# Six more load buffers in the expert stage of a two-layer trunk, except around the expert with split weights

## The chip, the core and the metric

The kernel runs on one core of a Trainium2 chip. The metric is the device time of one launch in microseconds, the median of several runs. The engines in what follows are PE (matmuls) with its weight load PEld, DVE, ACT and POOL (element-wise work), and SP, which here only issues DMAs and reads a few registers. Weights come from HBM by DMA and land in SBUF buffers.

## What is computed

The reference is a trunk of two layers on 256 tokens of width 1024. Each layer has a mixer (an mLSTM group beside an RG-LRU group) and a channel mixer: a dense SwiGLU in layer 0, eight experts in layer 1, of which each token uses two. The part that the change touches is the last:

```python
def _swiglu(h, w_gate, w_up, w_down):
    return (jax.nn.silu(h @ w_gate) * (h @ w_up)) @ w_down

def _moe(h, w_router, b_router, w_g, w_u, w_d):      # h 256 x 1024
    logits = (h @ w_router + b_router).astype(jnp.float32)
    top_v, top_i = lax.top_k(logits, TOP_K)           # 2 of 8
    top_p = jax.nn.softmax(top_v, axis=-1)
    gates = jnp.sum(jax.nn.one_hot(top_i, 8) * top_p[..., None], axis=-2)
    y = jnp.zeros_like(h)
    for e in range(8):                                # w_g[e], w_u[e] 1024 x 2816, w_d[e] 2816 x 1024
        y = y + gates[..., e:e + 1] * _swiglu(h, w_g[e], w_u[e], w_d[e])
    return y
```

All is float32; the eight experts hold 264 MiB of weights, and each weight is read once.

## The kernel before

**Units.** The weights are worked off in units of 128 x 2048 floats, 1 MiB (768 KB for the gate and up units of the last chunk of a tiled expert). The expert stage has 278 of them, numbered here from 0. `moe_units` (L551) lists them: for each expert and each chunk of its 2816 inner columns (1024, 1024, 768, or six chunks in the B expert) the gate units, the up units, and then the down units of the chunk before. PE works through them in this order: `gate_up` (L1459) and `down` (L1543) call `take` (L505) for each unit.

**Kinds.** `KINDS = "MSBMSMMS"` says how many tokens each expert may take: S 64, M 96, B 128. In S and M experts the matmuls read the loaded floats as they are (gate and up at L1471 in an S, L1478 in an M; down at L1580 in an S, L1561 in an M). Only expert 2, the B, uses split weights: `split` (L356) makes a high part `hi` on ACT and a low part `lo = raw - hi` on DVE, each 128 x 2048 floats, and PE makes three products of them (L1483 to L1485 for gate and up, L1583 to L1585 for down). Its units are 67 to 110 (those up to 75 mixed with the last downs of expert 1). Layer 0 and both mixers, before the expert stage, also use split weights, from a pool that is closed when the stage opens.

**Buffers.** A load goes into a buffer of `rawp` (6, `LOADS`) or, in the expert stage, of `rawx` (4, `EXTRA`). The pool `xs` has 3 buffers for `hi` and 3 for `lo`. All are of one size. `raws` (L320) lists the pools that loads may use, each with the number of its buffers and the units that it has taken. `fill` (L468) emits loads as long as a pool has room: a pool has room if the unit that used its next buffer is done with, which `free` (L465) decides, for a unit used as it is (work `whole`) by whether PE's instructions for it stand in the program, for a split unit by whether its split does. `advance` (L488) calls `fill` and splits up to two units ahead. So the order in which instructions are emitted decides which buffer a load takes and which wait it carries.

**Queues.** Each engine works through its instructions in order. The loads (one DMA for nearly every unit, L335) all stand on SP; a load whose buffer is still read blocks all behind it. It also waits on the semaphore (DMAHW0 to 7, in turn) of the DMA eight before it. Seven reads of expert numbers into registers (`places`, L1330, tile `eid`) stand on SP as well, since the address of an expert's weights from expert 1 on depends on the routing, and one read of `cnt` (L1777), which says whether some token found no place; the branch that handles that is not taken here.

The pools of the stage open at L1811:

```python
    with tc.tile_pool(name="ex", ...) as ep, tc.tile_pool(name="xs", bufs=3, ...) as xs, tc.tile_pool(name="rawx", bufs=EXTRA, ...) as rawx:
        raws.append((rawx, EXTRA, []))
        rt["splits"] = xs
        fill()
        moe(1, ep)
```

Of the kernel before, what the change touches and what calls it, by code (L numbers as in the profile page):

```python
# [8 lines left out]
F32 = mybir.dt.float32  # L9
# [7 lines left out]
P = 128  # L17
# [16 lines left out]
LOADS, SPLITS, EXTRA = 6, (2, 2, 2, 2), 4  # L34
# [90 lines left out]
def trunk(ctx: ExitStack, tc: tile.TileContext, I, out, dbg=None):  # L125
# [12 lines left out]
    rawp = ctx.enter_context(tc.tile_pool(name="rawp", bufs=LOADS))  # L138
# [177 lines left out]
    units, state = [], {"load": 0, "work": 0, "take": 0, "limit": 1 << 30, "phase": 0}  # L316
# [2 lines left out]

    raws = [(rawp, LOADS, [])]  # L320

    def load(ap, shape, pool=rawp):
        raw = pool.tile([P, 2048], F32, tag="raw", name="raw")
        if isinstance(ap, list):
            v = raw[:, :shape[0] * shape[1]].rearrange("p (a b) -> p a b", a=shape[0])
            for i, x in enumerate(ap):
                nc.sync.dma_start(v[i * 64:(i + 1) * 64], x)
            return v
        if len(shape) == 3:
            v = raw.rearrange("p (a b c) -> p a b c", a=shape[0], b=shape[1])  # L330
            for c in range(shape[0]):
                nc.sync.dma_start(v[:, c], ap[:, c])
            return v
        v = raw[:, :shape[0] * shape[1]].rearrange("p (a b) -> p a b", a=shape[0])
        nc.sync.dma_start(v, ap)  # L335
        return v
# [124 lines left out]
    def run_tails(upto_):  # L461
        while tails and tails[0][0] <= upto_:
            tails.pop(0)[1]()

    def free(j):  # L465
        return j < (state["take"] if units[j]["work"] is whole else state["work"])

    def fill():  # L468
        while state["load"] < len(units):
            room = [r for r in raws if len(r[2]) < r[1] or free(r[2][-r[1]])]  # L470
            if not room:
                break
            u = units[state["load"]]
            u["raw"] = load(u["ap"]() if callable(u["ap"]) else u["ap"], u["shape"], room[0][0])
            room[0][2].append(state["load"])
            state["load"] += 1
            n = len(vectors) if state["load"] <= 4 else 0
            for _ in range(min(5, n)):
                vectors.pop(0)()

    def work(n):
        for _ in range(n):
            u = units[state["work"]]
            u["work"](u)
            state["work"] += 1
            fill()

    def advance(i):  # L488
        while True:
            fill()  # L490
            if state["work"] >= min(state["load"], i + 1 + SPLITS[state["phase"]], state["limit"]):
                break
            work(1)
# [735 lines left out]
    def moe(l, ep):  # L1229
# [398 lines left out]
        def general(ov, e, xn, j):  # L1628
# [26 lines left out]
            for c0, n in groups["B"]:  # L1655
                res = []
                for nm in ("w_exp_gate", "w_exp_up"):
                    ps = bank("ps_gu2")
                    kk = 4 if n == 512 else 8
                    for k0 in range(0, KD, kk):  # L1660
                        w = I[nm][0, bass.ds(e, 1), k0 * P:(k0 + kk) * P, c0:c0 + n]
                        raw = load(w.rearrange("o (k p) f -> p (o k) f", p=P), (kk, n))
                        for i in range(kk):
                            TE.matmul(ps[:, :n], xg[:, k0 + i, :], raw[:, i, :], start=k0 + i == 0,
                                      stop=k0 + i == KD - 1)
                    res.append(ps)
                a = ov.tile([P, 512], F32, name="a2", tag="a2")
                S.activation(a[:, :n], res[0][:, :n], AF.Silu)
                V.tensor_mul(a[:, :n], a[:, :n], res[1][:, :n])
                pt = bank("ps_t2")  # L1670
                for c in range(n // P):
                    TE.transpose(pt[:, c * P:(c + 1) * P], a[:, c * P:(c + 1) * P], ident)
                aT = ov.tile([P, 512], F32, name="aT", tag="aT")
                V.tensor_copy(aT[:, :n], pt[:, :n])
                for f0 in range(c0, c0 + n, 256):
                    w = I["w_exp_down"][0, bass.ds(e, 1), f0:f0 + 256, :]
                    raw = load(w.rearrange("o (k p) f -> p (o k) f", p=P), (2, D))
                    for c in range(2):
                        f = f0 + c * P
                        for h2 in range(2):  # L1680
                            TE.matmul(yo[h2], aT[:, f - c0:f - c0 + P], raw[:, c, h2 * 512:(h2 + 1) * 512],
                                      start=f == 0, stop=f == DFF - P)
# [126 lines left out]
    splits[0].__exit__(None, None, None)  # L1809
    prep.__exit__(None, None, None)  # L1810
    with tc.tile_pool(name="ex", bufs=1, reuse_waits="tile") as ep, tc.tile_pool(name="xs", bufs=3, reuse_waits="tile") as xs, tc.tile_pool(name="rawx", bufs=EXTRA, reuse_waits="tile") as rawx:  # L1811
        raws.append((rawx, EXTRA, []))
        rt["splits"] = xs
        fill()
        moe(1, ep)
# [28 lines left out]
```

## Time and profile before

| | us |
|---|---|
| runs | 1250.68, 1253.91, 1261.38 |
| median | 1253.91 |
| profiled execution | 1259.08 |
| its span in the trace | 1257.3 |
| mean granted clock of PE over the span | 0.972 |
| PE busy | 1178.8 (94% of the span) |
| DVE, ACT busy | 591.9 (47%), 374.8 (30%) |
| loaded from HBM | 397.67 MB, 317 GB/s over the span |

The expert stage runs from about 490 us to the end. In the profile a busy row gives an engine, the line of the kernel, the operation, `out<-in` with the names of the tiles (buffer numbers left out), and, in brackets, how long the engine was idle before it and which instruction or DMA released it; `issue` means that nothing in the trace did. The granted clock is a share of full speed: 1.00 is 2.4 GHz, 0.50 is 1.2 GHz. A row that holds several instructions (x8) gives the time from the first one's start to the last one's end. Matmuls overlap by some tenths of a microsecond, so the distance of two units is read from the start of one to the start of the next.

### The profile page before, as it was taken

How to read it: one execution, taken by the hardware profiler on the slowest of the kernel's cores; microseconds unless marked ns; L12 is line 12 of the kernel's file. 1: busy time of each engine (PE TensorE's matmuls, PEld its weight loads, DVE VectorE, ACT ScalarE, POOL GpSimd, SP SyncE). 2: the span in 40 equal slices, each digit the busy share in tenths (PEclk: the TensorE clock that was granted, in tenths of full speed). 3: DMA queues.
4: the chain of work that ended last, by engine and by line, in shares of the span. 5: the costliest groups of instructions: out<-in, count | busy, mean ns of one | idle time of the engine just before them, and what ended most of it. 6: DMA issues, size and time to landing. Idle time of an engine off the chain costs nothing.

```text
span 1257.3 us, 27066 instructions
## 1 busy us (share of the span) xinstructions
PE 1178.8 (94%) x11763; PEld 889.2 (71%) x11763; DVE 591.9 (47%) x992; ACT 374.8 (30%) x576; POOL 20.7 (2%) x51
## 2 busy tenths in 40 slices
PE   2999999999999998999997999999998999899994
PEld 2899989999999988666544688757534576567531
DVE  6899889898669974211013588220100101010122
ACT  3482564443458542102002477100000001000101
POOL 4000000000010000000000000000000000000000
PEclk9999999999999998899998899999999999999998
DMA  9986749999847646598999999889999999999994
GB/s 307 345 261 231 256 172 371 364 312 329 269 126 239 210 154 234 215 327 336 343 404 400 394 393 398 314 303 386 356 405 408 408 404 374 359 320 398 343 404 172
DMA packets 152557, 400.54 MB, mean 319 GB/s; under 512 B 6920, under 2 KB 56384, under 8 KB 152432
## 3 DMA queue, kind: packets, MB, share of 16 engines
q1 hardware_dynamic: 151872, 397.59, 87.1%
q8 instruction: 94, 1.54, 0.5%
q0 software_dynamic: 560, 1.16, 0.3%
q14 instruction: 31, 0.25, 0.1%
HBM read 397.67 MB, written 1.05 MB: 317 GB/s over the span
## 4 chain that ended last, share of the span: by engine, by line
PE 84%; DMA 11%; ACT 2%; DVE 2%; issue 1%; SPq 0%; DVEq 0%; ACTq 0%
PE ps_y L1561 10%; PE ps_g L1478 6%; PE ps_gu L1478 6%; PE ps_z L663 6%; PE ps_z L662 6%; PE ps_z L664 6%; PE ps_u L1478 6%; DMA raw<-in_w_exp_gate_dram 4%; PE ps_g L1471 4%; PE ps_u L1471 3%; PE ps_acc L662 2%; PE ps_acc L664 2%; DMA raw<-in_w_exp_up_dram 2%; PE ps_acc L663 2%; PE ps_acc L835 2%; PE ps_xg L1446 2%
## 5 line engine op out<-in xcount | busy, mean ns | idle before, releaser
L114 DVE TENSOR_TENSOR lo<-raw,hi 128x2048 fp32r<-128x2048 f32 x93 | 211.2, 2286 | 41.0 <-ACT hi L114 25.1
L114 ACT CAST hi<-raw 128x2048 fp32r<-128x2048 f32 x92 | 174.5, 1904 | 90.5 <-PE ps_acc L663 26.5
L662 PE MATMUL ps_z<-hh,hi 128*128 128x256 f32 x624 | 176.6, 285 | 1.4 <-ACT hi L114 1.3
L663 PE MATMUL ps_z<-hl,hi 128*128 128x256 f32 x624 | 176.1, 283 | 0.1
L664 PE MATMUL ps_z<-hh,lo 128*128 128x256 f32 x624 | 175.2, 283 | 0.0
L1478 PE MATMUL ps_gu<-raw,xf 128*32 128x256 f32 (+1 forms) x1536 | 124.3, 364 | 2.8 <-issue 2.8
L114 DVE SCALAR_TENSOR_TENSOR a<-a,gs,ps_u 128x256 f32<-128x256 f32 (+3 forms) x39 | 20.5, 551 | 223.4 <-PE ps_u L1478 108.0
L1561 PE MATMUL ps_y<-raw,aT 128*32 128x256 f32 (+1 forms) x1584 | 121.5, 451 | 0.0
L662 PEld LDWEIGHTS ps_z<-hh,hi 128*128 128x128 f32 x624 | 118.9, 191 | 2.1 <-ACT hi L114 1.7
L663 PEld LDWEIGHTS ps_z<-hl,hi 128*128 128x128 f32 x624 | 118.8, 190 | 0.7 <-DVE hl L114 0.5
L664 PEld LDWEIGHTS ps_z<-hh,lo 128*128 128x128 f32 x624 | 118.1, 190 | 0.1
L1561 PEld LDWEIGHTS ps_y<-raw,aT 128*32 128x32 f32 x1584 | 75.0, 110 | 41.8 <-issue 3.5
L1478 PE MATMUL ps_g<-raw,xf 128*32 128x256 f32 (+1 forms) x1536 | 101.7, 368 | 2.0 <-DMA raw<-in_w_exp_gate_dram 2.0
L1478 PE MATMUL ps_u<-raw,xf 128*32 128x256 f32 (+1 forms) x1536 | 99.0, 362 | 3.0 <-issue 3.0
L114 DVE SCALAR_TENSOR_TENSOR acc<-raw,cond,acc 128x1024 f32<-128x1024 f32 x77 | 98.4, 1279 | 5.1 <-DMA raw<-in_w_ada_dram 3.8
L1478 PEld LDWEIGHTS ps_gu<-raw,xf 128*32 128x32 f32 x1536 | 58.7, 111 | 26.2 <-issue 4.4
L114 ACT COPY aT<-ps_t 128x512 f32<-128x512 f32 (+1 forms) x21 | 11.5, 550 | 219.0 <-PE ps_t L1536 143.7
L1478 PEld LDWEIGHTS ps_g<-raw,xf 128*32 128x32 f32 x1536 | 53.8, 111 | 29.3 <-issue 6.8
L1478 PEld LDWEIGHTS ps_u<-raw,xf 128*32 128x32 f32 x1536 | 56.1, 110 | 24.7 <-issue 4.8
L1580 PE MATMUL ps_y<-raw,aT 128*64 128x512 f32 x264 | 62.2, 599 | 9.3 <-DMA raw<-in_w_exp_down_dram 8.6
L1471 PE MATMUL ps_u<-raw,xf 128*64 128x512 f32 (+1 forms) x288 | 60.8, 562 | 2.3 <-DMA raw<-in_w_exp_up_dram 2.3
L1471 PE MATMUL ps_g<-raw,xf 128*64 128x512 f32 (+1 forms) x288 | 62.0, 563 | 0.8 <-DMA raw<-in_w_exp_gate_dram 0.8
(498 smaller groups left out, 1763.2 us busy)
## 6 DMA issues: line engine op xcount, KB each, us to landing
raw<-in_w_exp_down_dram SPq DMA_DIRECT2D x84, 1024.0 KB, 13.9
raw<-in_w_exp_gate_dram SPq DMA_DIRECT2D x67, 1024.0 KB, 10.0
raw<-in_w_exp_up_dram SPq DMA_DIRECT2D x67, 1024.0 KB, 13.8
raw<-in_w_ada_dram SPq DMA_DIRECT2D x40, 1024.0 KB, 6.9
raw<-in_w_in_dram SPq DMA_DIRECT2D x24, 1024.0 KB, 6.1
raw<-in_w_exp_gate_dram SPq DMA_DIRECT2D x28, 768.0 KB, 15.5
raw<-in_w_exp_up_dram SPq DMA_DIRECT2D x28, 768.0 KB, 6.5
raw<-in_w_ff_gate_dram SPq DMA_DIRECT2D x11, 1024.0 KB, 7.5
```

The source lines that it names most:

```text
L114: r = op(*a, **kw)
L662: TE.matmul(ps, wh, xh, start=first, stop=False, **kw)
L663: TE.matmul(ps, wh, xl, start=False, stop=False, **kw)
L664: TE.matmul(ps, wl, xh, start=False, stop=last, **kw)
L835: TE.matmul(out_, w[:, c, js], parts[c], start=start, stop=stop, skip_group_check=True)
L1446: TE.matmul(p, src[:, t, k * P:(k + 1) * P], oh[:, t, :w], start=n == 0 and t == 0, stop=n == 1 and t == 1)
L1471: TE.matmul(ps[0][b * 64:b * 64 + 64, :h], xf[:, k, :], w[:, q, b * h:(b + 1) * h], start=k == 0, stop=k == KD - 1)
L1478: TE.matmul(o[j * 32:j * 32 + 32], xf[:, k, g * 32:g * 32 + 32], w[:, q, j * h:(j + 1) * h], start=k == 0 and (g == 0 or g == 2 and key == ...
L1561: TE.matmul(y[bank_][r:r + 32, c:c + nd], x(g), w[:, b, d0:d0 + nd], start=first and start, stop=last, skip_group_check=True)
L1580: TE.matmul(y[0][h2 * 64:h2 * 64 + 64], ah[:, o + b * 64:o + b * 64 + 64], w[:, c, ns], start=first, stop=last)
```

## The change

The `hi` and `lo` buffers of the pool `xs` become two more entries of `raws`, three buffers each, under their own tags, so that a raw load may land in them: 16 buffers instead of 10. `load` gets the tag as an argument. `fill` uses these two entries only where `no_split` allows it: the unit to be loaded lies more than 8 ahead of the first split unit of the expert stage (so up to unit 58), or all splits have been emitted (`state["work"]` is past the last split unit, from the load of unit 118 on).

```diff
--- before.py
+++ after.py
@@ -319,8 +319,8 @@
 
     raws = [(rawp, LOADS, [])]
 
-    def load(ap, shape, pool=rawp):
-        raw = pool.tile([P, 2048], F32, tag="raw", name="raw")
+    def load(ap, shape, pool=rawp, tag="raw"):
+        raw = pool.tile([P, 2048], F32, tag=tag, name="raw")
         if isinstance(ap, list):
             v = raw[:, :shape[0] * shape[1]].rearrange("p (a b) -> p a b", a=shape[0])
             for i, x in enumerate(ap):
@@ -462,16 +462,22 @@
         while tails and tails[0][0] <= upto_:
             tails.pop(0)[1]()
 
+    def no_split(j):
+
+
+        i = [n for n, u in enumerate(units) if len(u["key"] or ()) == 4 and u["work"] is split]
+        return j < i[0] - 8 or j > i[-1] and state["work"] > i[-1]
+
     def free(j):
         return j < (state["take"] if units[j]["work"] is whole else state["work"])
 
     def fill():
         while state["load"] < len(units):
-            room = [r for r in raws if len(r[2]) < r[1] or free(r[2][-r[1]])]
+            room = [r for r in raws if (len(r[2]) < r[1] or free(r[2][-r[1]])) and (len(r) < 4 or no_split(state["load"]))]
             if not room:
                 break
             u = units[state["load"]]
-            u["raw"] = load(u["ap"]() if callable(u["ap"]) else u["ap"], u["shape"], room[0][0])
+            u["raw"] = load(u["ap"]() if callable(u["ap"]) else u["ap"], u["shape"], room[0][0], *room[0][3:])
             room[0][2].append(state["load"])
             state["load"] += 1
             n = len(vectors) if state["load"] <= 4 else 0
@@ -1809,7 +1815,7 @@
     splits[0].__exit__(None, None, None)
     prep.__exit__(None, None, None)
     with tc.tile_pool(name="ex", bufs=1, reuse_waits="tile") as ep, tc.tile_pool(name="xs", bufs=3, reuse_waits="tile") as xs, tc.tile_pool(name="rawx", bufs=EXTRA, reuse_waits="tile") as rawx:
-        raws.append((rawx, EXTRA, []))
+        raws.extend(((rawx, EXTRA, []), (xs, 3, [], "hi"), (xs, 3, [], "lo")))
         rt["splits"] = xs
         fill()
         moe(1, ep)
```

On PE, DVE, ACT and POOL the instructions stand in the order of before. On SP the DMAs are the same ones in the same order; what changes is which waits they carry, and where the register reads stand among them. In the rows, numbers behind names tell apart tiles of one name, and the semaphores named are those of DMA queues and of engines. The lines of the change are up to six lower in the file, so L1330 becomes L1336 and L1777 becomes L1783.

**SP where the stage opens, before.** The first row is the load of unit 8, the second of unit 9; `cnt` and `eid` are the results of the routing that DVE works out.

```order
L335 DMA raw_5535<-in_w_exp_gate_dram 128x2x1024 [waits DMAHW6_49]
L335 DMA raw_5537<-in_w_exp_gate_dram 128x2x1024 [waits DMAHW7_49]
L1777 TENSOR_LOAD cnt_5547 [waits DVE_49]
L1777 ISA x2
L1330 TENSOR_LOAD eid_5548 [waits DVE_49]
L1330 ISA x2
L1330 TENSOR_LOAD eid_5548
L1330 ISA x2
L1330 TENSOR_LOAD eid_5548
L1330 ISA x2
L335 DMA raw_5671<-in_w_exp_gate_dram 128x2x1024 [waits DMAHW0_49,PE_49]
```

The register reads of the routing stand behind ten loads, and unit 10's load (raw_5671) behind them waits for PE.

**The same place on SP now:**

```order
L335 DMA raw_5535<-in_w_exp_gate_dram 128x2x1024 [waits DMAHW6_49]
L335 DMA raw_5537<-in_w_exp_gate_dram 128x2x1024 [waits DMAHW7_49]
L335 DMA raw_5539<-in_w_exp_gate_dram 128x2x1024 [waits DMAHW0_49]
L335 DMA raw_5541<-in_w_exp_gate_dram 128x2x1024 [waits DMAHW1_49,PE_49]
L335 DMA raw_5543<-in_w_exp_up_dram 128x2x1024 [waits DMAHW2_49]
L335 DMA raw_5545<-in_w_exp_up_dram 128x2x1024 [waits DMAHW3_49]
L335 DMA raw_5547<-in_w_exp_up_dram 128x2x1024 [waits DMAHW4_49,Activation_49]
L335 DMA raw_5549<-in_w_exp_up_dram 128x2x1024 [waits DMAHW5_49]
L335 DMA raw_5683<-in_w_exp_down_dram 128x2x1024 [waits DMAHW6_49,PE_49]
L335 DMA raw_5709<-in_w_exp_down_dram 128x2x1024 [waits DMAHW7_49,PE_49]
L335 DMA raw_5735<-in_w_exp_down_dram 128x2x1024 [waits DMAHW0_49,PE_49]
```

Units 10 to 15 (raw_5539 to raw_5549) follow at once, their waits on PE and ACT belong to tiles of the stages before, and the reads of `eid` have moved behind 17 more loads, down the queue (L1336). The load of unit 16 (raw_5683) is the first that waits for a unit of this stage.

**SP after the B expert, before.** Seven rows from the load of unit 117; each ISA row works out an address.

```order
L335 DMA raw_8023<-in_w_exp_up_dram 128x2x1024 [waits DMAHW4_49,PE_49]
L335 ISA
L335 DMA raw_8029<-in_w_exp_up_dram 128x2x1024 [waits DMAHW5_49,DVE_49]
L335 ISA
L335 DMA raw_8055<-in_w_exp_down_dram 128x2x1024 [waits DMAHW6_49,PE_49]
L335 ISA
L335 DMA raw_8087<-in_w_exp_down_dram 128x2x1024 [waits DMAHW7_49,PE_49]
```

Each load but that of raw_8029 waits for PE, which must be done with the unit that lies ten before.

**SP after the B expert now,** eleven rows from the load of unit 117:

```order
L335 DMA raw_8023<-in_w_exp_up_dram 128x2x1024 [waits DMAHW4_49,PE_49]
L335 ISA
L335 DMA raw_8029<-in_w_exp_up_dram 128x2x1024 [waits DMAHW5_49]
L335 ISA
L335 DMA raw_8031<-in_w_exp_down_dram 128x2x1024 [waits DMAHW6_49]
L335 ISA
L335 DMA raw_8033<-in_w_exp_down_dram 128x2x1024 [waits DMAHW7_49,DVE_49,PE_49]
L335 ISA
L335 DMA raw_8035<-in_w_exp_down_dram 128x2x1024 [waits DMAHW0_49]
L335 ISA
L335 DMA raw_8037<-in_w_exp_down_dram 128x2x1024 [waits DMAHW1_49]
```

From unit 118 (raw_8029) on the six buffers are used again. raw_8033 (unit 120) waits for DVE and PE, that is for the last readers of unit 110's high part; raw_8035 to raw_8039 behind it carry no wait on PE.

**SP at the end of the program now,** the last two loads and what follows; `yacc` holds the output.

```order
L335 DMA raw_11367<-in_w_exp_down_dram 128x2x1024 [waits DMAHW6_49,PE_49]
L335 ISA
L335 DMA raw_11373<-in_w_exp_down_dram 128x2x1024 [waits DMAHW7_49,PE_49]
L1783 TENSOR_LOAD cnt_5559
L1783 ISA x2
L1632 DMA out_dram<-yacc_5551 128x512 [waits DMAHW0_49,Activation_49]
```

The read of `cnt`, which stood ahead of unit 10's load, now stands between the last load and the first store.

## Rows read from the trace of the kernel before

**Rows 1.** The page, part 4: share of each engine in the chain that ended last

```profile
PE 84%; DMA 11%; ACT 2%; DVE 2%; issue 1%; SPq 0%; DVEq 0%; ACTq 0%
```

**Rows 2.** Stretches: us, busy of PE PEld DVE ACT POOL, clock, DMA share, GB/s

```profile
490.00:515.00 25.00, 21.70 (x129) 15.67 (x132) 12.46 (x61) 7.20 (x13) 0.00 (x0) 0.53 0.41 165
490.00:1240.00 750.00, 717.22 (x8144) 443.67 (x8145) 174.13 (x293) 123.11 (x156) 0.60 (x1) 0.97 0.97 363
655.00:680.00 25.00, 18.16 (x96) 6.69 (x92) 2.76 (x2) 3.83 (x5) 0.00 (x0) 0.98 1.03 399
680.00:685.00 5.00, 4.80 (x11) 3.80 (x12) 4.86 (x10) 3.23 (x2) 0.00 (x0) 0.50 1.04 397
880.00:930.00 50.00, 50.00 (x319) 23.82 (x315) 7.01 (x14) 3.12 (x6) 0.00 (x0) 1.00 1.03 375
930.00:960.00 30.00, 23.79 (x153) 8.21 (x150) 0.61 (x1) 1.08 (x2) 0.00 (x0) 1.00 1.03 406
960.00:1043.00 83.00, 80.81 (x1374) 52.82 (x1374) 11.14 (x28) 6.47 (x13) 0.00 (x0) 1.00 1.03 406
1060.00:1156.00 96.00, 90.66 (x1582) 63.08 (x1574) 10.68 (x25) 4.82 (x10) 0.00 (x0) 1.00 0.98 349
1220.00:1242.00 22.00, 16.21 (x73) 4.29 (x67) 1.89 (x3) 1.07 (x2) 0.00 (x0) 1.00 0.76 303
```

**Rows 3.** Timeline 639 to 690: start, us, engine, line, operation, tiles, count, idle before

```profile
638.82 4.46 PE L1471 MATMUL ps_u<-raw,xf 128*64 128x512 f32 x20
645.88 7.09 PE L1580 MATMUL ps_y<-raw,aT 128*64 128x512 f32 x32
652.79 1.46 PE L1471 MATMUL ps_g<-raw,xf 128*64 128x384 f32 x8
654.77 4.09 PE L1471 MATMUL ps_g<-raw,xf 128*64 128x384 f32 x24
658.69 4.04 PE L1471 MATMUL ps_u<-raw,xf 128*64 128x384 f32 x24
675.92 1.90 ACT L114 CAST hi<-raw 128x2048 fp32r<-128x2048 f32 x1 [16.52 <-DMA raw<-in_w_exp_gate_dram]
677.87 0.51 PE L1483 MATMUL ps_g<-hi,xh 128*128 128x512 f32 x1 [2.72 <-ACT hi L114]
681.39 4.49 DVE L114 TENSOR_TENSOR lo<-raw,hi 128x2048 fp32r<-128x2048 f32 x2
688.24 0.39 PE L1483 MATMUL ps_u<-hi,xh 128*128 128x512 f32 x1
```

**Rows 4.** Timeline of PE at the last end: first and last of seven down units

```profile
1223.64 1.94 PE L1580 MATMUL ps_y<-raw,aT 128*64 128x512 f32 x8
...
1238.69 1.94 PE L1580 MATMUL ps_y<-raw,aT 128*64 128x512 f32 x8 [0.57 <-DMA raw<-in_w_exp_down_dram]
```

**Rows 5.** DMA issues in 625 to 660, then in 820 to 845: KB, median us to landing

```profile
raw<-in_w_exp_down_dram SPq DMA_DIRECT2D x7, 1024.0 KB, 15.0
...
raw<-in_w_exp_up_dram SPq DMA_DIRECT2D x2, 768.0 KB, 4.7
```

**Rows 6.** Timeline of PE at the end of expert 4, and at 986

```profile
930.68 1.46 PE L1471 MATMUL ps_g<-raw,xf 128*64 128x384 f32 x8
...
957.19 1.07 PE L1478 MATMUL ps_g<-raw,xf 128*32 128x256 f32 x16 [0.72 <-DMA raw<-in_w_exp_gate_dram]
...
986.01 1.07 PE L1478 MATMUL ps_g<-raw,xf 128*32 128x256 f32 x16 [1.30 <-DMA raw<-in_w_exp_gate_dram]
```

**Rows 7.** Timeline of PE: last matmul of unit 110

```profile
817.46 0.39 PE L1585 MATMUL ps_y<-hi,eal 128*128 128x512 f32 x1
```

**Rows 8.** The line that reads expert numbers: ns min/median/max, first and last start

```profile
L1330 SPq TENSOR_LOAD <-eid x7: 262/263/281, 510.8 to 544.8; - x7
```

**Rows 9.** Timeline of PE in expert 6: two stops with no releaser

```profile
1070.63 0.42 PE L1478 MATMUL ps_u<-raw,xf 128*32 128x256 f32 x4 [1.82 <-issue]
...
1080.41 0.42 PE L1478 MATMUL ps_gu<-raw,xf 128*32 128x256 f32 x4 [2.67 <-issue]
```

## The prediction

> **What bounds the kernel now.** I read the page first: its chain of work that ended last is 84% PE and 11% DMA [rows 1], and the DMA steps on it are expert weights. The change touches expert loads alone, so the question is where in the expert stage (from 490 us on) PE waits for them. The table of stretches answers that. PE is busy for all of 880 to 930, but only 18.16 of 25 us in 655 to 680, 23.79 of 30 in 930 to 960 and 16.21 of 22 in 1220 to 1242 [rows 2]. These three stretches are the ends of the three S experts (1, 4 and 7). The PE timeline shows why: a down unit of an S expert takes 6.91/4 = 1.73 us where nothing waits (645.88 to 652.79) [rows 3], while seven of them at the last end start 15.05/6 = 2.51 us apart, with a load named as releaser [rows 4]. At 406 GB/s, the rate of the fullest stretches [rows 2], 1 MiB takes 1.048576/0.406 = 2.58 us. So in an S expert PE eats faster than the transfers feed it, and it lives on what was loaded ahead; near its end that store is empty. In the M experts a unit takes PE about as long as its transfer, and the transfers pause whenever all ten buffers are full: only 165 GB/s in 490 to 515 and 349 in 1060 to 1156 [rows 2]. A larger store is filled in these pauses and spent in the S experts. That is what can be gained, and no more than PE's waits.
>
> **What the change does to the queues.** On PE, DVE, ACT and POOL each row of the program stands where it stood; only SP differs, so a saving can only come from a load that lands earlier. Sixteen buffers instead of ten mean that a load is issued when the unit sixteen before it is eaten. I cost the three places apart, counting units from 0 at expert 0's first gate unit; unit 67 is the first of expert 2 (the B), unit 110 its last.
>
> **First end, expert 1 to expert 2.** Ahead of it the store does fill: units 10 to 15 no longer wait for a unit of this stage, and the pause in 490 to 515, 25 x (406-165)/406 = 14.8 us [rows 2], is about the 6 x 2.58 = 15.5 us that six units need. From unit 59 on the rule gives the six buffers back; that load now waits until unit 48 is eaten, at 638.82 + 4 x 0.215 = 639.7 (the first four of the twenty matmuls in that row are its last) [rows 3], much as before. But before, the queue was so full that loads issued in 625 to 660 took 15 us to land [rows 5]; now it is empty at 639.7. Units 59 to 67 are 8 MiB (four are 768 KB): 639.7 + 8 x 2.58 + 2.8 = 663.1, where 2.8 is the 4.7 us of a 768 KB load that meets a short queue [rows 5] less its 1.94 of transfer. The split of unit 67 takes 1.90 on ACT and 4.49/2 = 2.25 on DVE [rows 3]: ready at 667.3. PE needs it later. Without waits the fourth up unit follows three that take 3.92 (as 654.77 to 658.69), so it starts at 662.61; 1.31 for it and 6.91 for four downs give 670.83 for the first matmul of unit 67, which started at 677.87 [rows 3]: 7.0 us. Then units 67 and 68 took 677.87 to 688.24, 10.37 us [rows 3], because the low part came late and the granted clock was 0.50, the 1.2 GHz level, in 680 to 685 [rows 2], after the idle stretch. At the full level I estimate 24 of their matmuls at 5.5 (0.23 each, as 688.24 and after), and the transposes and gate sums between them at 0.8. What stays is the split of unit 68, which stands behind a copy on ACT: its low part is done 2.25 after 681.39, at 683.6, 5.75 after unit 67's start, and PE wants it after 3.8, so 1.95 remains. 10.37 - 8.25 = 2.1. **Together 9.1.** Bounds: 7.0 less some 0.6, 6.4, if that remaining wait drops the clock again; 11 if it vanishes too. In expert 2 itself nothing changes, its loads go through ten buffers as now.
>
> **Second end, expert 4 to expert 5.** From 930.68 to 957.19 PE needed 26.5 us [rows 6] for what takes 652.79 to 670.83 = 18.0 in expert 1 without waits. **8.5 at most here**, and the cover is thin. The six buffers come back with unit 118, but SP is one queue, and unit 120 takes the slot of unit 110's high part, which PE reads until 817.5 [rows 7]. All behind it on SP waits until then; PE wants that unit only some 27 us later, so nobody is held up by it. From 817.5 on the loads follow without a pause. Units 120 to 170 are 47 MiB: 121.4 us at 2.58, plus 50 x (406-375)/406 = 3.8 for the slower stretch 880 to 930 [rows 2], plus 2.8 as above: 945.5, against 930.68 + 18.0 = 948.7 when PE wants unit 170. The margin is 3.2, or 1 at the 399 GB/s of 655 to 680 [rows 2]. I take 8.5; bounds 4 (transfers 6% slower: 128 x 0.06 = 7.7, of which the margin takes 3.2) and 9.8 (the 1.30 wait at 986 [rows 6] goes too).
>
> **Third end, expert 7.** Expert 6 leaves 96 x (406-349)/406 = 13.5 us of transfer time unused in 1060 to 1156 [rows 2]; six buffers take it up. The seven down units span 15.05 [rows 4] where 6 x 1.73 = 10.4 would do: **4.7**, bounds 3 (the store is 1 MiB short) and 5.1 (a little of the wait ahead of them as well). What follows the last unit is the same work.
>
> **What costs nothing.** Seven reads of expert numbers on SP move behind more loads; 0.26 us each [rows 8], in a queue that waits for PE there, and the first load that needs one is unit 32's. The read of cnt goes to the end of SP, behind the last load and ahead of the first store: SP has nothing to issue there for longer than one such read, since the last units must first be eaten and added up; bare it would be 0.26.
>
> **A rule against it.** The full stretches run at 399 to 406 GB/s [rows 2], and I go by them. The Trainium skill, HBM Reference, Specifications, gives about 358 GB/s as a core's share of memory bandwidth, and puts a core that streams alone well above it. The trace agrees with the second half, 406 on this one core; by the share alone the gain would be zero.
>
> **Sum.** 9.1 + 8.5 + 4.7 = 22.3 us. The profiled execution took 1259.1 us (its span is 1257.3), so it would take 1236.8; it lies 0.4% above the median of the three runs, 1253.9. Against the median: 1231.6.
>
> **Rivals.** *The second end is not gained:* the transfers come out a few per cent slower, or a slot is released later than I read. Then 9.1 + 4.7 = 13.8, so 1240. For it: a margin of 1 to 3 us after 128 us of transfers. Against: 406 GB/s in 930 to 960 and again over the 83 us of 960 to 1043 [rows 2]. Chance 0.14.
>
> *PE's stops multiply, and it gets slower.* In expert 6 PE stops twice with nothing named to wait for, 1.82 and 2.67 us, 9.8 us apart [rows 9]; the place is the M experts (0, 3, 5, 6), some 300 us in which the queue will now be full. If PE stopped 2.2 us every 10 us there, 66 us, the time would be 1298. It decides from 16 more such stops on (35 us, 1267). Against: in 960 to 1043, an M expert under a full queue, PE stands still 2.2 us in all [rows 2], of which 1.30 is a wait for a load [rows 6]. Chance 0.03 for slower, 0.06 that a few stops eat half the gain (1243). The Trainium skill, Runtime: NRT & Kernel Launch, Instruction fetch mechanics, says that an engine fetches its own program by DMA in 16 KiB blocks, mostly hidden: by that rule this rival costs nothing, while the trace names no cause for the two stops.
>
> *No transfer capacity:* over 490 to 1240 the mean is 363 GB/s [rows 2]. If that mean cannot rise, the last load lands where it does now: 1254. The 406 of the full stretches speaks against it; 0.03.
>
> *The buffers stand empty,* since an old tile under them is released late at 490: then the first end is lost, 13.2 remain, 1240.7; 0.02. The forecast, 1227 to 1236, has 0.68, and 0.04 is left for more (the two stops of rows 9 gone too, below 1227).
>
> **Numbers.** A change of this kernel shows from about 1% on, 12.5 us. Faster by that needs 1241.4 or less: the forecast 0.68, the upside 0.04, and 0.14 of the 0.16 of the first and last rivals: 0.86. Same: the other 0.02, half eaten by stops 0.06, no capacity 0.03: 0.11. Slower: 0.03. The range goes from 1223 (upper bounds 11 + 9.8 + 5.1 = 25.9, and the two stops, 4.5) to 1242 (lower bounds 6.4 + 4 + 3 = 13.4, with 1 us for spread).
>
> **What would show it.** Right: at the ends of experts 1, 4 and 7 the down units of PE 1.73 us apart with no load as releaser; unit 67 starting some 31 us after unit 48 is eaten, not 38; no pause of transfers in 490 to 515; clock 1.0 where it was 0.50 at 680; SP held at unit 120 until unit 110 is eaten, then loads in a burst. Wrong: the 2.5 us spacing still there at the second end, or new stops of PE without releaser in experts 0, 3 and 5.

## The result

| | before | the change |
|---|---|---|
| median of four runs, us | 1255.64 | 1238.48 |
| lowest to highest | 1250.68 to 1261.38 | 1236.27 to 1239.70 |
| profiled execution (span) | 1259.08 (1257.3) | 1239.35 (1237.6) |

The ratio of the times is 0.986, with a 95% interval of 0.981 to 0.991: 17.2 us faster, and inside the predicted range of 1223 to 1242, but 6.9 us above the predicted time. Measured once more (below, the last run), the change gave 1237.48 against 1256.55, ratio 0.985 (0.982 to 0.988).

In the profile of the change the chain of work that ended last has less DMA than in [rows 1]:

```profile
PE 85%; DMA 8%; DVE 3%; ACT 3%; issue 1%; SPq 0%; DVEq 0%; ACTq 0%
```

The table of stretches (columns as in [rows 2]) shows where the stage changed, and where it did not:

```profile
490.00:515.00 25.00, 21.70 (x132) 17.71 (x135) 12.01 (x57) 8.29 (x16) 0.00 (x0) 0.62 0.88 345
600.00:655.00 55.00, 55.00 (x376) 26.61 (x370) 6.94 (x14) 3.12 (x6) 0.00 (x0) 1.00 0.89 334
655.00:680.00 25.00, 23.60 (x126) 11.74 (x123) 8.74 (x12) 8.97 (x7) 0.00 (x0) 1.00 1.03 392
680.00:685.00 5.00, 5.00 (x21) 3.21 (x20) 2.06 (x1) 0.60 (x1) 0.00 (x0) 1.00 1.01 393
820.00:1200.00 380.00, 375.12 (x4911) 226.48 (x4909) 51.19 (x109) 28.01 (x55) 0.60 (x1) 1.00 1.03 387
1045.00:1058.00 13.00, 11.17 (x217) 7.14 (x213) 0.16 (x1) 0.60 (x1) 0.00 (x0) 0.87 1.03 226
```

The pause at the start of the stage is mostly filled, 345 GB/s at a DMA share of 0.88 in 490 to 515 where [rows 2] has 165 at 0.41. In 655 to 680 PE is busy 23.60 of 25 us (18.16 before), and in 680 to 685 its clock is 1.00 (0.50 before). In 820 to 1200 the DMA engines are busy without a break (share 1.03), and yet they move 387 GB/s and not 406; in 1045 to 1058 it is 226. That row is the key to what was forecast wrongly.

The ends of the three S experts on the PE timeline of the change, against [rows 3, 4, 6]. First the end of expert 1, then that of expert 4, then that of expert 7 (on the lines of the change, L1586 is the S down, L1477 the S gate and up, L1489 and L1490 the B gate and up):

```profile
665.15 7.04 PE L1586 MATMUL ps_y<-raw,aT 128*64 128x512 f32 x32
...
672.11 0.51 PE L1489 MATMUL ps_g<-hi,xh 128*128 128x512 f32 x1
...
677.71 0.50 PE L1490 MATMUL ps_g<-lo,xh 128*128 128x512 f32 x1 [1.38 <-DVE lo L114]
...
932.27 7.04 PE L1586 MATMUL ps_y<-raw,aT 128*64 128x512 f32 x32
939.75 1.07 PE L1484 MATMUL ps_g<-raw,xf 128*32 128x256 f32 x16 [0.45 <-DMA raw<-in_w_exp_gate_dram]
...
1204.14 1.94 PE L1586 MATMUL ps_y<-raw,aT 128*64 128x512 f32 x8
1206.47 1.94 PE L1586 MATMUL ps_y<-raw,aT 128*64 128x512 f32 x8 [0.40 <-DMA raw<-in_w_exp_down_dram]
...
1219.13 1.94 PE L1586 MATMUL ps_y<-raw,aT 128*64 128x512 f32 x8 [0.56 <-DMA raw<-in_w_exp_down_dram]
```

At the first two ends four down units stand in one row of 7.04 us, 1.76 each, with no wait for a load between them; ahead of expert 2 the wait for the low part of unit 68 stays, 1.38 us (677.71), where 1.95 was forecast. At the third nothing has changed in this profile: units start 2.3 to 2.6 us apart, a load is the releaser, and from the first to the last of the seven it is 1219.13 - 1204.14 = 14.99 us where [rows 4] gives 15.05. The change has a second profile (the last run below); there the same distance is 13.48 us.

Counted from unit to unit (start of the first matmul of each on the PE timeline) the stage shrank as follows:

| from the first matmul of ... to that of ... | before, us | change, us | difference | forecast |
|---|---|---|---|---|
| unit 0 to 59 (expert 0, start of 1) | 151.8 | 149.2 | -2.6 | 0 |
| unit 59 to 75 (end of expert 1) | 52.1 | 41.5 | -10.6 | -9.1 |
| unit 75 to 170 (expert 2 to end of 4) | 246.4 | 238.2 | -8.2 | -8.5 |
| unit 170 to 251 (experts 5, 6, start of 7) | 227.5 | 223.9 | -3.6 | 0 |
| unit 251 to 277 (rest of expert 7) | 54.0 | 55.5 | +1.5 | -4.7 |
| unit 0 to 277 | 731.8 | 708.3 | -23.5 | -22.3 |

The sum of the stage came out near the forecast, by errors that cancel. The spans differ by 19.7 only, since unit 0 starts at 510.8 in this profile and at 506.9 before. Over all kernels below that start lies anywhere from 505.8 (sixteen buffers, loads at half height) to 511.1, and at 510.2 in the run whose program is as before up to unit 117 (the six buffers only after expert 2), so the later start needs nothing of the change. Nor is a single profile the median: that of before lay 3.4 us above its own, that of the change 0.9, and so the medians differ by 17.2.

### The profile page after: what moved, and what is told of

Read it like the earlier page. It is cut to its first block, busy times and chain, and to the rows that moved or that the text cites. A ratio compares the mean times of both kernels' runs of the same rounds, so it can differ in the third digit from the quotient of the medians.

```text
span 1237.6 us, 27056 instructions
## 1 busy us (share of the span) xinstructions
PE 1171.2 (95%) x11763; PEld 888.0 (72%) x11763; DVE 592.1 (48%) x992; ACT 375.0 (30%) x576; POOL 20.3 (2%) x51
## 4 chain that ended last, share of the span: by engine, by line
PE 85%; DMA 8%; DVE 3%; ACT 3%; issue 1%; SPq 0%; DVEq 0%; ACTq 0%
PE ps_y L1567 9%; PE ps_g L1484 6%; PE ps_gu L1484 6%; PE ps_u L1484 6%; PE ps_z L668 6%; PE ps_z L670 6%; PE ps_z L669 6%; PE ps_g L1477 4%; PE ps_u L1477 4%; DMA raw<-in_w_exp_gate_dram 3%; PE ps_y L1586 3%; PE ps_acc L841 2%; PE ps_acc L668 2%; PE ps_acc L670 2%; PE ps_acc L669 2%; PE ps_xg L1452 1%
## 5 line engine op out<-in xcount | busy, mean ns | idle before, releaser
L1586 PE MATMUL ps_y<-raw,aT 128*64 128x512 f32 x264 | 60.8, 596 | 3.6 <-DMA raw<-in_w_exp_down_dram 2.9
L1477 PE MATMUL ps_g<-raw,xf 128*64 128x512 f32 (+1 forms) x288 | 61.6, 562 | 0.0
L1477 PE MATMUL ps_u<-raw,xf 128*64 128x512 f32 (+1 forms) x288 | 60.3, 560 | 1.3 <-DMA raw<-in_w_exp_up_dram 1.3
```

Source lines behind the costliest of these rows:

```text
L1477: TE.matmul(ps[0][b * 64:b * 64 + 64, :h], xf[:, k, :], w[:, q, b * h:(b + 1) * h], start=k == 0, stop=k == KD - 1)
L1586: TE.matmul(y[0][h2 * 64:h2 * 64 + 64], ah[:, o + b * 64:o + b * 64 + 64], w[:, c, ns], start=first, stop=last)
```

## The experiments

Two theories stood at the outset. The first: each end pays for itself, and the third end did not gain because transfers are the bound from 817 us on, some of them at half the rate. The rival: the store that PE eats up at one end is missing at the next, so the gains hang together.

**The two halves apart.** The six buffers only up to unit 58, and only after expert 2:

```diff
-        return j < i[0] - 8 or j > i[-1] and state["work"] > i[-1]
+        return j < i[0] - 8
```

```diff
-        return j < i[0] - 8 or j > i[-1] and state["work"] > i[-1]
+        return j > i[-1] and state["work"] > i[-1]
```

> The six buffers take loads only up to unit 58, never after expert 2. Theory (each end pays for itself: the first end 10.6 us as the trace of the change shows it): about 1245, the ends of experts 4 and 7 as long as before (26.5 and 15.05 us). Rival (the gain is passed on, since PE that is earlier finds fewer units ahead of it later): part of the 10.6 is lost again at the end of expert 4, which then takes 30 us or more, and the time is 1248 to 1252.

> The six buffers take loads only after expert 2. Theory (each end pays for itself): the first end as before, the second end 7 to 8 us shorter, the third not shorter, expert 6 without one of its two stops (up to 2.7): 1245 to 1247, so that the two halves add up to the whole. Rival (transfers bound the stage from 817 us on, and what is not gained at the first end is gained at the third): the third end is shorter as well, 1241.

Measured: 1249.52 and 1246.90, both beside 1257.80 for the kernel before, ratios 0.992 (0.988 to 0.995) and 0.991 (0.988 to 0.993). That is 8.3 and 10.9 us, together 19.2, and the whole gave 17.2 and, measured again, 19.1: within the intervals the halves add up. The first run is slower than the 1245 that was expected and lies in the rival's range, but not for the rival's reason: in its trace the end of expert 1 is as short as in the change, and the end of expert 4 (units 160 to 170) takes 22.7 us, as before (22.8) and no longer. In the second run it is the other way round (units 59 to 67: 20.0 us, units 160 to 170: 15.3). The first matmul behind each end that was not helped, in the first run (expert 5) and in the second (expert 2), still waits, for a load and for the split of a late load:

```profile
950.25 1.07 PE L1484 MATMUL ps_g<-raw,xf 128*32 128x256 f32 x16 [0.73 <-DMA raw<-in_w_exp_gate_dram]
```

```profile
681.80 0.71 PE L1489 MATMUL ps_g<-hi,xh 128*128 128x512 f32 x1 [2.70 <-ACT hi L114]
```

The third end takes 15.0 us in both. So the first two ends are independent, and the third gains from neither half.

**The loads at half height.** In the change the transfers drop to 216 to 240 GB/s once for each of the four M experts, for 8 to 14 us (590 to 598, 870 to 879, 1045 to 1059, and 1135 to 1152 in two pieces); the 13 us of the expectation below hold for the third alone. That is where the third down unit of an M expert's last chunk is loaded (units 42, 145, 215 and 250), the only one that is two loads of 64 partitions each. The edit makes it one load of 128 partitions, once on the change and once on the kernel before (PE then multiplies wrong rows):

```diff
-                            w = w.rearrange("(a b r) f -> b r a f", a=2, b=2)
-                            return [w[b, P:] for b in range(2)]
+                            return w[m * 256:(m + 1) * 256].rearrange("(k p) f -> p k f", p=P)
```

> The change, with one thing other: the third down unit of the last chunk of each M expert, now two loads of 64 partitions each, is one load of 128 partitions from the 256 rows that follow each other; PE then multiplies wrong rows, so this part of the result is not the reference's. Theory (these half-height loads run at half the rate for 13 us in each M expert, and transfers are the bound from 817 us to the last load): the stretches at 210 to 230 GB/s go, the third end loses its waits, 6 to 8 us, 1231. Rival (the rate falls for another reason, or the third end is held by something else than transfers): within 2 us of the change, 1237 to 1240.

> The kernel before with the same edit to that load (wrong rows multiplied there) and ten buffers. Theory: the first two ends are as before, since the queue was full ahead of them with ten buffers; the third, which has such a load close ahead of it, loses most of its 4.7 us: 1250 to 1252. Rival (the rate falls for another reason): 1255. If all three ends shrink, the buffers were needed only to cover these loads: 1245.

Measured: 1229.54 on the change, some 9 us less than the change alone, and the third end shrinks to 11.2 us. On the kernel before 1240.33, ratio 0.986 (0.983 to 0.988): as much as the six buffers bring. This was a miss, 1250 to 1252 was expected. There the first end became 2.7 us shorter (units 59 to 67: 19.2 to 16.5), the second 4.4 (units 160 to 170: 22.8 to 18.4), the third 3.9, and units 205 to 251 in experts 5 and 6 took 124.9 instead of 130.0. So the slow loads are felt at every end. An explanation, argued only, is that a queue that was full when the slow loads began is not full behind them.

**Height or pieces.** The unit stays two loads from rows that follow each other, once at 64 partitions, once at 128:

```diff
-                            w = w.rearrange("(a b r) f -> b r a f", a=2, b=2)
-                            return [w[b, P:] for b in range(2)]
+                            return [w[m * 256 + b * P:m * 256 + (b + 1) * P].rearrange("(a r) f -> r a f", a=2) for b in range(2)]
```

```diff
-                nc.sync.dma_start(v[i * 64:(i + 1) * 64], x)
+                nc.sync.dma_start(v[:, i], x)
...
-                            w = w.rearrange("(a b r) f -> b r a f", a=2, b=2)
-                            return [w[b, P:] for b in range(2)]
+                            return [w[m * 256 + b * P:m * 256 + (b + 1) * P] for b in range(2)]
```

> The change, with the third down unit of the last chunk of an M expert loaded as two loads of 64 partitions, as now, but from rows that follow each other (wrong rows are multiplied there). Theory (the half height sets the rate): as the change, a stretch of some 13 us at 210 to 230 GB/s in expert 6, 1238. Rival (the scattered rows in memory set it): no such stretch, 1230.

> The same unit as two loads of 512 KB again, from rows that follow each other, but each over all 128 partitions (wrong rows are multiplied there). Theory (the half height sets the rate): no stretch at 210 to 230 GB/s, 1230, as with one load. Rival (two smaller loads in place of one set it): as the change, 1238.

The same 14 us of the two traces, at 64 partitions first, then at 128:

```profile
1041.00:1055.00 14.00, 12.84 (x257) 7.97 (x259) 0.87 (x3) 0.82 (x2) 0.00 (x0) 1.00 1.03 244
```

```profile
1041.00:1055.00 14.00, 14.00 (x279) 9.74 (x280) 0.87 (x3) 1.08 (x2) 0.00 (x0) 1.00 1.03 409
```

Half height gives 244 GB/s with the DMA engines busy all the time (share 1.03), full height 409. It is the height, not the number of loads, and not where the rows lie. The times were 1235.15 and 1231.91, one run each. From unit 0 to unit 277 the first takes 709.0 us and the second 700.4, against 708.3 for the change and 700.3 for the edit to one load.

**The same at the right rows.** The last chunk of an M expert is turned in another way, so that its three down units are rows that follow each other and load at full height. Three transposes per group of columns become four, of the 64 columns that are used (the load's special case goes, and the copies and addresses behind the transposes follow; not shown):

```diff
-                for g in range(3):
-                    TE.transpose(p1[:, g * P:(g + 1) * P], a[:, g * 192:g * 192 + P], ident)
-                for g in range(3):
-                    c, x = slice(g * P, (g + 1) * P), a[:, g * 192 + P:(g + 1) * 192]
-                    TE.transpose(p2[:64, c], x, ident)
-                    turned_to(p2[64:, c], x)
...
+                for g in range(3):
+                    pick_to(p1[:, g * 64:g * 64 + 64], a[:, g * 192:g * 192 + P], 0)
+                    pick_to(p1[:, 192 + g * 64:256 + g * 64], a[:, g * 192 + 64:(g + 1) * 192], 1)
+                    pick_to(p2[:64, g * 64:g * 64 + 64], a[:, g * 192 + P:(g + 1) * 192], 0)
+                    pick_to(p2[64:, g * 64:g * 64 + 64], a[:, g * 192:g * 192 + 64], 1)
```

Here `pick_to` is a matmul with every other block of 32 columns of the identity.

> The change, and the last chunk of an M expert turned in another way, so that all three of its down units are loaded at full height from rows that follow each other, and the right rows are multiplied: per chunk twelve transposes of 64 columns take the place of nine of 128, and one copy of two. Theory (all the half-height loads cost is gone at no price): as with the wrong rows, 1229 to 1231, 25 us below the kernel before. Rival (the turning is on the path and costs some tenths for each of four M experts): 1231 to 1233.

> The kernel before with the same turning and loads, ten buffers. Theory: 1240, as with the wrong rows; beside the run above it the six buffers are worth 10 to 11 us once all loads run at the full rate. Rival (the buffers only covered the slow loads): 1232, no difference between the two.

Measured: 1230.13 on the change, ratio to the kernel before 0.977 (0.973 to 0.981), and 1240.89 with ten buffers, ratio 0.988 (0.984 to 0.992). Both as expected: the turning costs nothing that shows, and beside it the six buffers are worth 10.8 us. The change with these loads beats both kernels. Its stretches, and its third end, which is now two rows of four and three units, 1206.44 to the end of the last with no load as releaser:

```profile
820.00:1195.00 375.00, 374.28 (x4981) 226.87 (x4975) 50.02 (x106) 28.24 (x55) 0.60 (x1) 1.00 1.02 405
1037.00:1075.00 38.00, 38.00 (x682) 30.05 (x679) 3.24 (x8) 2.91 (x6) 0.00 (x0) 1.00 1.02 406
```

```profile
1198.71 7.09 PE L1581 MATMUL ps_y<-raw,aT 128*64 128x512 f32 x32
1206.44 5.42 PE L1581 MATMUL ps_y<-raw,aT 128*64 128x512 f32 x24 [0.63 <-ACT aT L114]
```

PE is busy 374.28 of 375 us and the transfers run at 405 GB/s throughout: with the slow loads gone PE hardly waits from expert 3 to the last end, and the transfers have little left as well (share 1.02 of 1.03).

**Three buffers instead of six,** and the change once more beside it:

```diff
-        raws.extend(((rawx, EXTRA, []), (xs, 3, [], "hi"), (xs, 3, [], "lo")))
+        raws.extend(((rawx, EXTRA, []), (xs, 3, [], "hi")))
```

> The change with only the three buffers of high parts as extra, 13 in all. Theory (buffers are worth the pauses of the transfers that they fill; with 16 the transfers still stand still some 9 to 10 us in 600 to 655, and before expert 4 the pause that is left to fill is under 5 us, so three units are enough): both ends gained as with six, 1238 to 1241. Rival (each buffer pays in proportion): half of it, 1247.

> The change as it is, once more beside the kernel before on the same chip. Theory (the expert stage is 22 to 24 us shorter, and the start of the stage moves by a few us from run to run): 17 to 22 us faster, and a start of the stage within 505 to 511 us. Rival (the change itself delays the start of the stage by 4 us): start at 510 or later, as in the first profile of it.

Measured: 1237.50 with three and 1237.48 with six, both beside 1256.55 (ratios 0.985, 0.982 to 0.988 each). Three buffers do all that six do. Units 59 to 67 take 12.4 us with three and 12.1 with six, units 160 to 170 15.8 and 14.7. The row of 600 to 655 with three buffers says why:

```profile
600.00:655.00 55.00, 55.00 (x374) 26.48 (x369) 6.93 (x14) 3.12 (x6) 0.00 (x0) 1.00 1.01 372
```

Share 1.01, so nothing pauses there, while with six the share is 0.89 in the same stretch (second row of the table of the change): the store is full at 600 and the last three buffers hold units that nobody would have waited for. By that share the pause with six is (1.03 - 0.89)/1.03 x 55 = 7.5 us; the 9 to 10 of the expectation went by GB/s. In its second profile the change starts the stage at 508.7, against 510.8 in its first, so the rival of a start delayed by the change is out.

The third end of the run with three buffers is short, 11.20 us, although the loads at half height are still there:

```profile
1205.43 7.09 PE L1586 MATMUL ps_y<-raw,aT 128*64 128x512 f32 x32
1213.15 5.42 PE L1586 MATMUL ps_y<-raw,aT 128*64 128x512 f32 x24 [0.63 <-ACT aT L114]
```

The time went to experts 5 and 6 instead: units 205 to 251 take 129.7 us there, 127.2 in the first profile of the change. The half-height run has the same 11.20.

## Why the prediction was right, and where it was wrong

**First end: right; what came beyond it is the clock.** Unit 67 was to come 7.0 us earlier, and units 59 to 67 shrank from 19.2 to 12.1 us, by 7.1. Units 67 and 68 were to take 8.25 us instead of 10.37, and took 8.23, in the second profile of the change 8.22. In the run with the buffers only after expert 2 they take 9.87, with no buffer ahead of them, so most of this saving is the buffers'. The table has 1.5 us more than the forecast of 9.1, and that is luck of the two profiles: units 69 to 75 took 22.5 us before and 21.2 in the change, but 19.7 in the run with the buffers only after expert 2 and 19.6 in the second profile of the change. In 695 to 715 the granted clock is 0.83 before, 0.91 in the first profile of the change and 1.00 in these two.

**Second end: right.** Forecast 8.5, measured 8.2 over units 75 to 170, in the second profile 7.7. The thin cover held: unit 170 waits 0.45 us. SP did stop at unit 120 until unit 110 was eaten (its last matmul ends at 808.69, the load goes at 808.72) and then sent its loads in a burst. Here the down loads of units 119 to 122 are spread over 9.52 us, and the next four loads go in 2.26:

```profile
801.68 9.52 SPq L335 DMA_DIRECT2D raw<-in_w_exp_down_dram  x4
811.39 2.26 SPq L335 DMA_DIRECT2D raw<-in_w_exp_gate_dram  x4
```

**Third end: wrong, term and reason.** It took the 349 GB/s of 1060 to 1156 as 13.5 us of transfer time unused that six more buffers would take up. The row itself says otherwise: its DMA share is 0.98 [rows 2]. The engines were not idle there, they were slow. Worked out from the share, before had left very little unused after 817:

```profile
817.00:1239.00 422.00, 403.47 (x5174) 235.76 (x5174) 52.90 (x112) 29.87 (x58) 0.60 (x1) 1.00 1.00 373
```

The full share is 1.03, so (1.03 - 1.00)/1.03 x 422 = 12.3 us in the whole rest of the program. From unit 111 (817.8 before, 808.6 after) to unit 277 (1238.7 and 1219.1) the change saved 420.9 - 410.5 = 10.4 of them, and 12.3 in its second profile, where the forecast had 8.5 + 4.7 = 13.2. In the first profile they were spent at the second end and in experts 5 and 6, and for the third nothing was left. Where the rest of the waiting falls differs from run to run, at the third end (15.0, 13.5) or ahead of it (11.2 with three buffers). What the runs agree on is the sum: with the loads at half height and buffers added after expert 2, units 111 to 277 take 408.6 to 410.6 us in five profiles, with all loads at full height and sixteen buffers 399.3 to 400.1 in three. In these three the third end takes 11.2 us, the 10.4 of the forecast but for a wait of 0.63 on a copy.

The Trainium skill, SBUF — State Buffer, "Can I just issue two DMAs to hit both halves?", says that two loads to the two halves of the partitions serialize, and that only one load over all 128 reaches all ports; its table above that section gives some 218 GB/s as the limit of 64 partitions. The trace comes near that rate, 226 GB/s in 1045 to 1058, and adds that the loads beside them are slowed too: 13 us at 226 GB/s are 2.9 MB, nearly three units, of which one is loaded at half height. Of the 714 packets of 4 KB that start in this stretch at most 256 are that unit's, and yet all but one took over 200 ns; in the run with two loads at full height 99.6% of those in 1041 to 1055 took less. That one unit costs 13 x (406 - 226)/406 = 5.8 us of transfer time. In PE's time the three such units after unit 111 cost some 10 us together (410.5 against 400.0 from unit 111 to 277).

**The number.** The miss of 6.9 us is not the third end alone, since the stage shrank by 1.2 us more than forecast in the profile. The other errors made up for the 6.2 of expert 7: 2.6 in expert 0, 1.5 at the first end and 3.6 in experts 5 and 6, less 0.3 at the second end. The 6.9 are what lies outside units 0 to 277, in the main the later start of the stage (23.5 - 19.7 = 3.8), the profiles that lie above their medians (2.6) and the median of before that rose from 1253.91 to 1255.64 (1.7), less these 1.2. That the time fell into the range is in part luck.

**What was costed at nothing.** Experts 5 and 6 gained 3.6 us that were not forecast; the two stops of [rows 9] make 4.49 us, the one that is left 1.83 (last section), which is 2.7 of it. In the second profile both stops are there again (1.82 and 1.57), and the gain is 1.8. The 2.6 of expert 0 are no effect of the buffers: units 0 to 59 take 149.2 to 149.7 us in some profiles and 151.3 to 151.8 in others, 151.8 in the first run above, which has the buffers there, and 149.3 in the run with rows in order and ten buffers. What differs is the clock: in 587 to 591 it is 0.58 before and 1.00 in the change. The moved register reads cost nothing that can be seen.

**The rivals.** That transfers have no capacity beyond their mean did not come, since the same loads went through in 708.3 us instead of 731.8 (unit 0 to 277), but it was near the truth after expert 2: the change has none left in 820 to 1200 (share 1.03). That PE's stops multiply did not come.

## What to carry to other kernels

Read unused transfer time from the busy share of the DMA engines, never from GB/s alone: low GB/s at a full share are slow loads, and more buffers do not make them faster. More load buffers are worth the pauses that they fill and no more; here three filled them, and three others bought nothing. Look for loads that cover half the partitions before buying buffers: with those four units loaded at full height the ten buffers of before gave as much as sixteen did without.

## What the runs showed of the hardware

While a unit is loaded over 64 partitions at a time, all transfers together run at little more than half the rate, 226 to 244 GB/s against 406 to 409, at a full busy share: the loads in flight beside it are slowed with it.

PE's stops without a releaser go with these stretches. In the change one is left of the two in [rows 9]:

```profile
1052.33 0.62 PE L1484 MATMUL ps_u<-raw,xf 128*32 128x256 f32 x4 [1.83 <-issue]
```

It lies inside 1045 to 1058, the stretch at 226 GB/s. From 1000 us on, all seven profiles of kernels with loads at half height (before, the change twice, its two halves, the half-height run, the three buffers) have one to three such stops of 0.75 to 2.67 us, nearly all during a slow stretch or within 5 us of its end; one of 0.85 in before, at 1141.5, is neither. The five profiles with loads at full height have none above 0.3 us there, though one has a stop of 0.79 at 864.8. What PE waits for is named in no row, but the traces speak for its own program. The pages list a queue `q8 instruction` with 94 packets of 16 KB, 250 instructions for each if they bring PE's 11763 matmuls and as many weight loads. Count PE's matmuls from 0: in all seven profiles a stop stands ahead of matmul 9901, and in five of them one ahead of matmul 10029, whatever the time is by then. Between the two lie 128 matmuls, 256 instructions with their weight loads, about one packet. Each of the stops, the 0.85 and the 0.79 included, ends 1.3 to 1.5 us after a packet of q8 does; in the change the packet takes 1049.66 to 1051.03 and PE goes on at 1052.33. In the run on the change with one load at full height the same packet is through 72 matmuls ahead of 9901, and there is no stop. The packet itself is little slower (1.37 us against 1.11), it starts later in the program, at matmul 9886 and not 9808. Why it starts late, behind the slow loads in the queues of the DMA engines or otherwise, no run tried.
